# A decoder layer on one core: scores of two groups sooner, output weights on GpSimd's queue, loads behind masks, the last blocks' order pinned

## The chip, the cores and the metric

The kernel runs on one core of a Trainium2 chip. A core has a matrix engine (TensorE, PE in the profile; its weight loads are PEld), VectorE (DVE), ScalarE (ACT), GpSimd (POOL) and SyncE (SP). They run side by side, each through its own list of instructions in order, and wait for each other by semaphores. Transfers are issued by SP, POOL or ACT in the order of their lists and are carried by 16 DMA engines. The metric is the device time of one execution in microseconds. The kernel before takes 1504.59 us, the median of three runs (1503.69 to 1505.47).

## What is computed

One layer of a decoder: 4096 new tokens of one prompt, and 8 samples with 8 tokens each against caches. A norm, one wide projection, three groups of heads, one output projection, a second norm and the residual sum:

```python
h = _rmsnorm(x, g_pre)
z = h @ w_in                                    # 4096+64 tokens, 1024 -> 2816
cb, cc, ch, cg, q, k, v, ag, mq, mg = _split_cols(z)
...
out_a = jax.nn.silu(cg) * cb * conv             # conv of 3 tokens over cc * ch, 256 channels
o_b, new_k, new_v = _window_prompt(q, k, v, sink_g)   # 8 heads, window 128, in blocks of 128 queries
out_b = jax.nn.silu(ag) * o_b
o_c = _mem_attend(mq.reshape(n, t, MEM_HEADS, HEAD_DIM), mem_k, mem_v)   # 4 heads, 256 memory tokens
out_c = jax.nn.silu(mg) * o_c
y = jnp.concatenate([out_a, out_b, out_c], axis=-1) @ w_out
return x + _rmsnorm(y, g_post), new_conv, new_k, new_v
```

All is float32. Each factor is split into a high and a low part of a shorter format, and a product is three passes (high by high, low by high, high by low).

## The kernel before

The input projection runs in three phases over the columns of w_in. Here only phase 2 matters (669 to 955 us): 8 blocks of 520 tokens, and for each block seven products p = 0 to 6 in place of eight (a Strassen-like scheme over a 2 x 2 split). A step is one product of one block; the text counts them n = 7 (b - 1) + p from block 1 on, so n = 30 is block 5, product 2. A step is 36 matmuls of 128 x 260 (line 374). For each step SP loads the tile x (x_5T, x_6B, x_7T, ...: block and place in the scheme), ACT casts it to hi (line 364), DVE takes the difference lo (line 365), and DVE adds the finished product into z (evictions, line 381). DVE also forms gates (line 417) and turns values (vq, line 851).

On these steps third_jobs hangs other work. The prompt's attention is cut into 32 groups of 128 queries, two to a chunk of 256; a chunk has its keys kst, queries q (chunk_load: one load of kst and two of q on GpSimd's queue) and its mix, the gated rows into which the attention is multiplied (load_mix). The first three groups are worked on during phase 2: pieces 0 to 3 are their scores (ws for the window, xs for the memory, on PE; softmax on ACT and DVE), then the turn (a transpose in 32 x 32 squares on DVE and 16 transfers w<-s that move the squares), the masks (four GpSimd instructions on w, into w and wd), and the values (pv on PE). The table EARLY gives the step of each piece, a row to a group.

Then come blocks i = 0 to 32 of attention and output projection, 128 tokens each (32 is the samples): 48 matmuls y<-wo with events hung between them, each at a place (half of the columns, k of 8). Block i holds the scores of group i + 3, its turn, the masks of group i + 2 and, at its start, the values of group i + 1. Behind the matmuls follow the norm (ACT squares, DVE, the root by pow on GpSimd, ACT scales) and the sum with x (xr, on GpSimd). The samples' attention is spread over blocks 26 to 30 by the table sample: sample_window has the stages load and mask, then sws and svnt (scores and the turning of new values) with their softmax, then swt (the turned weights), then swo. Its mask tile smask and the masked weights wd of even groups lie in one slot (wp[0]), which one of them holds at a time.

What sets the order: phases 0 and 1 are written out by hand. From phase 2 on a scheduler orders each engine's instructions by what it takes to be ready first; only what is marked (keep_in_program_order, or everything of an engine while the InOrder flags are set: DVE and PE in all blocks before the last, POOL in blocks 1 and 2, ACT in block 0) stays in the order of the program. Slots of a pool are given to whoever is scheduled first. w_out is loaded by wo_load in eight pairs (wor) into slots that the last weights and tiles of phase 2 leave, and wo_split splits it (ACT casts, DVE or GpSimd subtracts, line 197).

## Time and profile before

| | us |
|---|---|
| median of three runs | 1504.59 |
| the profiled execution | 1505.62 |
| its span, first to last instruction | 1503.9 |
| PE busy in the span | 1470.2 (98%) |
| DVE busy | 1211.9 (81%) |
| ACT busy | 758.0 (50%) |
| POOL busy | 441.8 (29%) |
| mean granted PE clock | 0.992 of full |

Times in the trace count from the first instruction. A row of waits names the engine and the line that stood still, then the instruction or transfer that ended it. Line 66 is a helper through which most instructions of the blocks are recorded, so they are told apart by their tiles. A name such as pv<-w,vh means that pv is written from w and vh; buffer numbers are left out. SPq and POOLq are the issuing queues. The PE clock is granted by the chip in parts of full speed.

### The profile page before, as it was taken

To read this page: it belongs to the slowest core of one execution; us is meant where nothing else is said; L and a number is where in the kernel's file an instruction comes from. 1 tells how busy PE (TensorE), PEld (TensorE's weight loads), DVE (VectorE), ACT (ScalarE), POOL (GpSimd) and SP (SyncE) were. 2 spreads that over 40 slices of the span, in tenths; PEclk is the share of its full clock that TensorE was granted. 3 is DMA by queue.
4 is the path that set the end of the run, shared out by engine and by line. 5 is a ranking of instruction groups with operands and counts; after the bars stand their busy time and mean duration, and the time that the engine had idled before them with its cause. 6 is when DMAs were issued, how large, how long until landed. Compare 5 with 4: busy or idle time off the path is not lost.

```text
span 1503.9 us, 30849 instructions
## 1 busy us (share of the span) xinstructions
PE 1470.2 (98%) x11459; PEld 1343.8 (89%) x11459; DVE 1211.9 (81%) x1889; ACT 758.0 (50%) x1869; POOL 441.8 (29%) x607
## 2 busy tenths in 40 slices
PE   9999999999999999999999999889999999999988
PEld 9999999999999999999999889767777777777756
DVE  6779888899988777797667767969888988889833
ACT  6776566465422222254534435656556566556531
POOL 0223233212300000000003213355665565666531
PEclk9999999999999999999999999999999999999989
DMA  9989999887854333478877988898899988898662
GB/s 258 196 234 227 287 294 266 249 262 264 236 197 165 120 114 115 146 247 290 288 233 210 273 255 261 293 254 213 231 238 239 235 220 214 222 242 211 190 203 78
DMA packets 213756, 337.26 MB, mean 224 GB/s; under 512 B 55270, under 2 KB 126822, under 8 KB 213574
## 3 DMA queue, kind: packets, MB, share of 16 engines
q1 hardware_dynamic: 169973, 259.23, 57.5%
q0 software_dynamic: 42336, 72.91, 20.1%
q10 hardware_dynamic: 1296, 3.15, 0.6%
q8 instruction: 91, 1.49, 0.4%
q14 instruction: 60, 0.48, 0.1%
HBM read 192.48 MB, written 110.15 MB: 201 GB/s over the span
## 4 chain that ended last, share of the span: by engine, by line
PE 77%; DMA 6%; issue 6%; DVE 6%; ACT 2%; SPq 1%; POOL 1%; ACTq 0%; POOLq 0%; DVEq 0%
PE c L374 49%; PE y L66 18%; PE pv L66 4%; PE ws L66 2%; DMA w<-s 1%; PE xs L66 1%; DMA place<-md 1%; PE mem_acc L789 1%; SPq L1234 1%; ACT s L1193 1%; DMA x_5T<-hd_T 1%; DMA wr_3S<-sd6S 1%; DMA o_yp<-xr 1%; DMA vd<-v 1%; DMA x_7B<-hd_B 0%
## 5 line engine op out<-in xcount | busy, mean ns | idle before, releaser
L66 PE MATMUL y<-wo,mh 128*128 128x512 f32 x992 | 319.2, 396 | 0.0
L381 DVE TENSOR_TENSOR z<-c,z 128x520 f32<-128x520 f32 (+1 forms) x308 | 194.5, 644 | 93.7 <-PE c L374 92.5
L66 PEld LDWEIGHTS y<-wo,mh 128*128 128x128 f32 x992 | 187.1, 189 | 52.3 <-DVE wmx L66 5.4
L66 PE MATMUL y<-wo,ml 128*128 128x512 f32 x496 | 194.0, 391 | 0.0
L1193 ACT ACTIVATE s<-s,wnm 128x128 f32<-128x128 f32 x248 | 96.0, 388 | 47.8 <-DVE wnm L66 42.8
L1217 POOL TENSOR_SCALAR s<-s,xrd 128x256 f32<-128x256 f32 x120 | 57.5, 493 | 199.0 <-DVE xrd L66 104.0
L66 PEld LDWEIGHTS y<-wo,ml 128*128 128x128 f32 x496 | 93.6, 189 | 18.3
L1178 ACT COPY s<-ws 128x256 f32<-128x256 f32 x124 | 40.0, 378 | 94.0 <-PE ws L66 70.5
L748 POOL MEMSET negs<- 128x1 f32 x1 | 0.1, 99 | 266.7 <-PE c L374 266.7
L1565 POOL TENSOR_TENSOR xr<-yn,xr 128x1024 f32<-128x1024 f32 x29 | 69.6, 2400 | 21.6 <-ACT yn L1564 21.4
L66 DVE STREAM_TRANSPOSE s<-s 128x1024 f32<-128x1024 f32 x58 | 71.0, 1237 | 3.1 <-POOL s L1217 2.9
L1248 POOL TENSOR_SCALAR_AFFINE_SELECT wd<-w 128x512 f32<-128x512 f32 (+1 forms) x60 | 53.8, 896 | 49.2 <-DMA w<-s 30.7
L1545 ACT ACTIVATE y<-y 128x512 f32<-128x512 f32 (+1 forms) x64 | 37.4, 584 | 51.4 <-DVE yn L66 44.5
L66 DVE TENSOR_TENSOR yn<-y,gpost 128x512 f32<-128x512 f32 x62 | 42.3, 682 | 22.8 <-PE y L66 21.6
L1209 ACT ACTIVATE s<-xs,xnm 128x256 f32<-128x256 f32 x124 | 56.4, 462 | 5.5 <-DVE xnm L1207 4.8
L66 DVE COPY_PREDICATED s<-wmask,ws 128x256 f32<-128x256 uint8 x116 | 45.0, 440 | 15.3 <-ACT s L1178 5.5
L66 PEld LDWEIGHTS ws<-kst,q 64*128 64x128 f32 x696 | 43.1, 186 | 12.9 <-issue 12.9
L66 PE MATMUL ws<-kst,q 64*128 64x256 f32 x696 | 49.1, 287 | 2.7 <-issue 2.7
L383 ACT COPY z<-c 128x520 f32<-128x520 f32 (+1 forms) x44 | 24.4, 554 | 51.9 <-PE c L374 49.3
L1248 POOL TENSOR_SCALAR_AFFINE_SELECT w<-w 128x512 f32<-128x512 f32 x60 | 48.9, 834 | 1.8
L1564 ACT ACTIVATE yn<-yn,yst 128x1024 f32<-128x1024 f32 x31 | 35.7, 1150 | 27.0 <-POOL yst L1558 24.6
L287 ACT ACTIVATE nat<-nat 104x1024 f32<-104x1024 f32 x40 | 42.2, 1055 | 11.4 <-DMA nat<-in_x_p 11.4
(999 smaller groups left out, 5019.1 us busy)
## 6 DMA issues: line engine op xcount, KB each, us to landing
w<-s SPq DMA_DIRECT2D x464, 64.0 KB
q<-qd POOLq DMA_DIRECT2D x32, 768.0 KB, 8.8
xr<-in_x_p SPq DMA_DIRECT2D x32, 512.0 KB
nat<-in_x_p SPq DMA_DIRECT2D x39, 416.0 KB
o_yp<-xr SPq DMA_DIRECT2D x31, 512.0 KB
md<-th POOLq DMA_DIRECT2D x48, 260.0 KB, 6.8
qd<-zh SPq DMA_DIRECT2D x48, 260.0 KB
qd<-z SPq DMA_DIRECT2D x48, 260.0 KB
```

The costliest lines, as they stand in the source:

```text
L66: return (lambda *args, **kw: tc.keep_in_program_order(fn(*args, **kw))) if on else fn
L287: S.activation(t[:RG], t[:RG], AF.Square, accum_out=r[:RG, i : i + 1])
L374: TE.matmul(bank[:, :HW], l, r, start=first and i == 0, stop=last and i == 3 * KH - 1)
L381: add = lambda dst, other: V.tensor_tensor(dst, c, other, op=ALU.add)
L1178: S.copy(to, squares(s3[:, :, P : 2 * P]))
L1193: S.activation(sm[:, h], sm[:, h], AF.Exp, bias=nm[:, h : h + 1], scale=SCALE, accum_out=den[:, h : h + 1])
L1209: S.activation(p[:, i], s[:, i].rearrange("p (a k j) -> p a k j", a=2, k=4), AF.Exp, bias=nm[:, i : i + 1], scale=SCALE, accum_out=den[:, ...
L1217: G.tensor_scalar(p[:, i], p[:, i], rd[:, i : i + 1], 0.5, op0=ALU.mult, op1=ALU.mult)
L1248: G.affine_select(out, src, pattern=[[32 * sign, 2], [0, 8], [sign, 32]], compare_op=op, fill=0.0, base=base * sign, channel_multiplier=-s ...
L1545: square = lambda acc=acc, p=p, c0=c0, c1=c1, end=end: S.activation((psum(2, "sq") if end else acc)[:m, : c1 - c0], acc[:m], AF.Square, sc ...
L1564: tc.keep_in_program_order(S.mul(yn, yn, st[:, 3:4]))
L1565: G.tensor_tensor(self.xr, yn, self.xr, op=ALU.add)
```

## The change

Five things are changed.

1. EARLY: group 0's turn, masks and values come one, two and two steps sooner; all pieces of group 1 three to five steps sooner; those of group 2 six to eight. Chunk 1's load goes from step 29 to step 26.
2. wo_load issues on GpSimd's queue instead of SP's, and the last split goes from GpSimd to DVE.
3. Chunk 3's keys and queries, and chunk 2's mix, are asked for behind the masks of group 3 in block 1; the mix goes from SP's queue to GpSimd's.
4. In blocks 28 to 30 the root and the sum on GpSimd stay in the order of the program.
5. sample_window's second stage goes from the first half of block 28 to its second.

```diff
-        if n == 29:
-            jobs.append(lambda: chunk_load(1))
         for b, at in enumerate(EARLY):
...
+        if n == 26:
+            jobs.append(lambda: chunk_load(1))
...
-    EARLY = ((15, 16, 17, 18, 20, 24, 26), (25, 26, 27, 28, 30, 34, 36), (36, 37, 38, 39, 41, 45))
+    EARLY = ((15, 16, 17, 18, 19, 22, 24), (22, 23, 24, 25, 26, 29, 31), (30, 31, 32, 33, 34, 37))
...
-            DMA.dma_start(wo_raw[j + n], a["w_out"][k + n][:, 512 * h : 512 * h + 512])
+            G.dma_start(wo_raw[j + n], a["w_out"][k + n][:, 512 * h : 512 * h + 512])
...
-        w_split(wo[k][h], wo_raw.pop(j), G if j > 8 and j % 2 else V)
+        w_split(wo[k][h], wo_raw.pop(j), G if j in (9, 11, 13) else V)
...
-            DMA.dma_start(self.mix, md[:, :, self.ts].rearrange("k p n -> p k n"))
+            (G if self.c == 2 else DMA).dma_start(self.mix, md[:, :, self.ts].rearrange("k p n -> p k n"))
...
-        if i in (1, 2):
-            chunk_load(i + 2)
+        if i == 2:
+            chunk_load(4)
...
-                G.tensor_tensor(st[:m, 3:4], st[:m, 3:4], mhalf[:m, 0:1], op=ALU.pow)
+                root = G.tensor_tensor(st[:m, 3:4], st[:m, 3:4], mhalf[:m, 0:1], op=ALU.pow)
+                if 28 <= b < 31:
+                    tc.keep_in_program_order(root)
...
-                    G.tensor_tensor(self.xr, yn, self.xr, op=ALU.add)
+                    total = G.tensor_tensor(self.xr, yn, self.xr, op=ALU.add)
+                    if 28 <= b < 31:
+                        tc.keep_in_program_order(total)
...
-              (27, 0, 3): window, (28, 0, 6): window, (29, 0, 4): window, (30, 0, 3): window}
+              (27, 0, 3): window, (28, 1, 3): window, (29, 0, 4): window, (30, 0, 3): window}
...
-        elif (i + 3) // 2 < NCH - 1:
+        elif 1 < i and (i + 3) // 2 < NCH - 1:
             at(0, 3, lambda: chunks[(i + 3) // 2].load_mix())
         at(1, 1, turn, 2, i + 2)
+        if i == 1:
+            at(1, 1, chunk_load, 3)
+            at(1, 1, lambda: chunks[2].load_mix())
```

How the instructions stand, at three places. At the start of step 39 PE had two pieces of group 2's memory scores between the products; they are gone from there, and the first matmul that needs lo_6T follows the two high ones at once.

ScalarE in steps 45 to 48, before; hi are the casts of the tiles of steps 45 to 48, wo the casts of the output weights:

```order
L364 CAST hi_7T_11766<-x_7T_11644 128x1040
L364 CAST hi_7T_11821<-x_7T_11707 128x1040
L193 CAST wo_0_11783<-wor_11727 128x512
L193 CAST wo_0_11799<-wor_11727 128x512
L193 CAST wo_0_11816<-wor_11743 128x512
L193 CAST wo_0_11843<-wor_11743 128x512
L193 CAST wo_0_11859<-wor_11761 128x512
L193 CAST wo_0_11862<-wor_11761 128x512
L364 CAST hi_7B_11885<-x_7B_11764 128x1040
L193 CAST wo_0_11902<-wor_11879 128x512
L364 CAST hi_7T_11943<-x_7T_11819 128x1040
```

And after:

```order
L364 CAST hi_7T_11771<-x_7T_11649 128x1040
L193 CAST wo_0_11788<-wor_11732 128x512
L193 CAST wo_0_11804<-wor_11732 128x512
L193 CAST wo_0_11821<-wor_11748 128x512
L364 CAST hi_7T_11826<-x_7T_11712 128x1040
L193 CAST wo_0_11843<-wor_11748 128x512
L193 CAST wo_0_11859<-wor_11766 128x512
L193 CAST wo_0_11862<-wor_11766 128x512
L364 CAST hi_7B_11885<-x_7B_11769 128x1040
L193 CAST wo_0_11902<-wor_11879 128x512
```

Three of the six weight casts now stand ahead of the tile of step 46 (hi_7T) and three behind it, ahead of hi_7B of step 47. The tiles' loads on SP's queue, which stood around the weights' loads, follow each other directly; the weights' loads stand on GpSimd's queue behind group 2's masks and ahead of the splits and of q and kst of chunk 2.

GpSimd from group 3's last weights on, before (L1217 and L66 TENSOR_SCALAR are the memory weights of groups 3 and 4, wd and w the masks of group 3):

```order
L66 TENSOR_TENSOR yst_12175<-yst_12175,mhalf 128x1
L66 TENSOR_TENSOR xr_12168<-yn_12174,xr_12168 128x1024
L66 DMA kst_12423<-qd 128x2x384
L66 DMA q_12425<-qd 128x6x256 x2
L66 TENSOR_SCALAR s_12351<-s_12351,xrd_0_12450 128x2x4x32 x2
L66 TENSOR_SCALAR s_12351<-s_12351,xrd_1_12458 128x2x4x32 x2
L66 AFFINE_SELECT wd_12508<-w_12334 128x512
L66 AFFINE_SELECT wd_12508<-w_12334 64x512
L66 AFFINE_SELECT w_12334<-w_12334 128x2x256 x2
```

And after:

```order
L66 TENSOR_SCALAR s_12351<-s_12351,xrd_0_12445 128x2x4x32 x2
L66 TENSOR_SCALAR s_12351<-s_12351,xrd_1_12453 128x2x4x32 x2
L66 AFFINE_SELECT wd_12502<-w_12334 128x512
L66 AFFINE_SELECT wd_12502<-w_12334 64x512
L66 AFFINE_SELECT w_12334<-w_12334 128x2x256 x2
L66 DMA kst_12507<-qd 128x2x384
L66 DMA q_12509<-qd 128x6x256 x2
L66 DMA place<-md 128x8x256
```

Keys and queries of chunk 3 have moved from the front of group 4's weights to behind group 3's masks, and the mix (place<-md) has come to this queue behind them.

GpSimd in blocks 28 and 29, before: the cast of smask, weights of group 31, masks of group 30, root (yst) and sum (xr) of block 28, root of block 29, masks of group 31 around the sum of block 29:

```order
L1426 CAST smask<-smraw 128x768
L1217 TENSOR_SCALAR s_18017<-s_18017,xrd_0_18112 128x2x4x32 x2
L1217 TENSOR_SCALAR s_18017<-s_18017,xrd_1_18120 128x2x4x32 x2
L1248 AFFINE_SELECT wd_18238<-w_17970 128x512
L1248 AFFINE_SELECT wd_18238<-w_17970 64x512
L1248 AFFINE_SELECT w_17970<-w_17970 128x2x256 x2
L1558 TENSOR_TENSOR yst_18015<-yst_18015,mhalf 128x1
L1565 TENSOR_TENSOR xr_17677<-yn_18014,xr_17677 128x1024
L1558 TENSOR_TENSOR yst_18294<-yst_18294,mhalf 128x1
L1248 AFFINE_SELECT wd_18387<-w_18248 128x512
L1248 AFFINE_SELECT wd_18387<-w_18248 64x512
L1565 TENSOR_TENSOR xr_17893<-yn_18293,xr_17893 128x1024
```

And after:

```order
L1248 AFFINE_SELECT wd_18193<-w_17970 128x512
L1248 AFFINE_SELECT wd_18193<-w_17970 64x512
L1248 AFFINE_SELECT w_17970<-w_17970 128x2x256 x2
L1426 CAST smask<-smraw 128x768
L1558 TENSOR_TENSOR yst_18015<-yst_18015,mhalf 128x1
L1567 TENSOR_TENSOR xr_17677<-yn_18014,xr_17677 128x1024
L1248 AFFINE_SELECT wd_18387<-w_18203 128x512
L1248 AFFINE_SELECT wd_18387<-w_18203 64x512
L1248 AFFINE_SELECT w_18203<-w_18203 128x2x256 x2
L1558 TENSOR_TENSOR yst_18294<-yst_18294,mhalf 128x1
```

The cast of smask now stands behind the masks of group 30, where the slot makes it wait for PE's last product of group 30's values, and the masks of group 31 stand ahead of block 29's root.

## The prediction

> **What bounds the kernel now.** I read the page first, then the waits of TensorE (PE), then the time in stretches, then single stretches of each queue.
>
> ```profile
> PE 1470.2 (98%) x11459; PEld 1343.8 (89%) x11459; DVE 1211.9 (81%) x1889; ACT 758.0 (50%) x1869; POOL 441.8 (29%) x607
> ```
>
> PE is busy for 98% of the span and no other engine comes near, and the change neither adds nor removes a matmul. So it can only move the time in which PE stands still, and the time in which PE runs slowly. Its waits that this change can reach lie in two places. From 800 to 1000 us, steps 20 to 48 of the input projection and the first blocks (waiting engine and line, what ended the wait, us in total, times, longest):
>
> ```profile
> PE pv L66 <- DMA w<-s: 4.8, 1, 4.8
> PE ws L66 <- issue: 2.7, 1, 2.7
> PE c L374 <- DVE lo_5B L365: 2.4, 1, 2.4
> PE c L374 <- DVE lo_7B L365: 1.5, 1, 1.5
> PE c L374 <- DVE lo_5T L365: 1.5, 2, 0.8
> PE c L374 <- ACT hi_7B L364: 0.9, 1, 0.9
> PE c L374 <- DVE lo_6T L365: 0.7, 1, 0.7
> PE c L374 <- DVE lo_7T L365: 0.6, 1, 0.6
> ```
>
> and from 1420 to 1466 us, the last blocks:
>
> ```profile
> PE pv L66 <- POOL w L1248: 5.9, 1, 5.9
> PE svnt L66 <- ACT s L1209: 0.7, 1, 0.7
> ```
>
> Between the two PE is full (second row below), while the stretch of the early groups is the one where the DMA engines are busiest for long (columns: window, length, busy time and count of PE, PEld, DVE, ACT, POOL, then PE clock, DMA share, GB/s):
>
> ```profile
> 800.00:880.00 80.00, 76.09 (x631) 73.26 (x630) 58.97 (x96) 33.44 (x71) 27.78 (x51) 0.98 0.91 267
> 1000.00:1424.00 424.00, 422.77 (x3063) 332.19 (x3061) 376.01 (x659) 252.53 (x920) 248.93 (x317) 1.00 0.89 226
> ```
>
> Each longer wait is paid a second time: behind it the granted clock falls to a half. The same view of PE alone, cut at the places where the clock changes (window, length, PE busy, PE clock, DMA share, GB/s):
>
> ```profile
> 871.09:874.51 3.42, 3.42 (x18) 0.53 1.12 278
> 939.36:942.77 3.41, 1.81 (x13) 1.00 1.03 389
> 942.77:946.19 3.42, 2.65 (x12) 0.53 1.03 380
> 946.19:949.60 3.41, 3.41 (x18) 0.50 0.36 120
> 993.97:997.39 3.42, 2.92 (x22) 0.53 0.74 208
> 1427.47:1430.88 3.41, 3.41 (x13) 0.52 0.80 232
> 1458.19:1461.60 3.41, 0.48 (x3) 0.52 0.11 44
> 1461.60:1465.00 3.40, 3.40 (x18) 0.50 0.44 139
> ```
>
> The clock changes on a grid of 3.41 us. A piece of the grid with only 1.81 us of PE work, 1.6 idle, is followed by one at half clock. PE work done at half clock costs half its busy time extra.
>
> **What each place loses today.** Wait plus half of the slow work: steps 30–33: 2.4 + 1.5 + 1.7 = 5.6; step 39: 0.7; steps 46–47: 0.6 + 0.9 + 1.5 + (2.65 + 3.41)/2 = 6.0; scores of group 4: 2.7; values of group 3: 4.8 + 1.5 = 6.3; sample window: 0.7 + 1.7 = 2.4; values of group 31: 5.9 + (0.48 + 3.40)/2 = 7.8. Together 31.5 us.
>
> **The change part by part.**
>
> *Earlier scores.* Group 1 moves by three steps or more, group 2 by six, group 0's masks and values by two. Their DVE and ACT work leaves steps 30–33, so the waits for lo_5T and lo_5B there (5.6) and lo_6T (0.7) go. Something takes its place. In step 39 VectorE has the same order today (eviction, turned values, then lo_6T), and PE waits so little because two pieces of group 2's scores stand ahead:
>
> ```profile
> 903.96 0.62 PE L1046 MATMUL xs<-mk,q 64*128 64x256 f32 x6
> 905.24 0.39 PE L374 MATMUL c<-lo_6T,w_0S 128*128 128x260 f32 x1 [0.66 <-DVE lo_6T L365]
> ```
>
> These move to step 33, and without them the wait grows to 0.66 + 2 × 0.62 = 1.9, say 2.1 (between 0.7 and the 2.4 of lo_5B, nearest to the sum); 1.6 us idle in one piece was enough above, so one piece at half clock follows, 1.7. In step 36 lo_6B comes behind evictions and both transposes of group 2; between 0 and 2.4 I take 0.7, as for lo_6T. Gain 6.3 − 4.5 = 1.8, ends −1 and 6.3. GpSimd's 16 turn transfers now run sooner:
>
> ```profile
> 810.79 6.99 POOL L1234 DMA_DIRECT2D w<-s  x14 [5.61 <-DVE s L1229]
> ...
> 824.19 1.54 POOL L1248 TENSOR_SCALAR_AFFINE_SELECT wd<-w 128x512 f32<-128x512 f32 x2 [4.04 <-DMA w<-s]
> ```
>
> They take 13.4 us to the masks. The first two matmuls of step 24, behind which the values of group 0 now stand, are
>
> ```profile
> 820.76 0.29 PE L374 MATMUL c<-hi_4T,w_0S 128*128 128x260 f32 x1
> 820.88 0.28 PE L374 MATMUL c<-lo_4T,w_0S 128*128 128x260 f32 x1
> ```
>
> A step has 36 such matmuls 0.12 us apart, 4.3 us. Issued one step sooner the transfers end at about 820 and the masks (824.19 to about 827 today) at 823, against PE at 821 to 824 within the step: 0 to 2 us of wait, I take 0. Chunk 1's load (two q, one kst on the same queue) is moved ahead of group 1's turn and three steps sooner; nobody needs it before step 30.
>
> *Output weights on GpSimd.* SyncE's queue today:
>
> ```profile
> 925.11 1.67 SPq L525 DMA_DIRECT2D x_7T<-hd_T  x1
> 926.86 5.72 SPq L909 DMA_DIRECT2D wor<-in_w_out  x6
> 932.63 0.44 SPq L525 DMA_DIRECT2D x_7B<-hd_B  x1
> ```
>
> The tile of step 47 (x_7B) stands behind six weight issues. After the change it follows x_7T directly, 5.7 us sooner, and the first six weight loads wait for step 42 only, so that ScalarE's weight casts no longer all stand between hi_7T and hi_7B and need not wait for their loads. What is left of 6.0 lies between 0 and 6.0; three casts and three splits still come ahead of hi_7B and lo_7B, so I leave 1.0 and gain 5.0. GpSimd waits in these issues for slots, but only q2, kst2 and three splits are behind them, and q2 waits for the end of step 48 in any case. One of the splits moves from GpSimd to VectorE. I cost it at nothing, since the 2.7 us wait for chunk 2's keys, which no part of the change touches, comes right behind and covers it; without that cover it costs its own length, at most.
>
> [...] If what holds x_7T and x_7B is the DMA engines (share 1.03 in two rows above), this part gains nothing: that is the first rival.
>
> *Chunk 3's loads and chunk 2's mix behind masks 3.* Today SyncE issues group 3's turn in one stretch:
>
> ```profile
> 972.56 17.53 SPq L1234 DMA_DIRECT2D w<-s  x16
> ```
>
> Among SyncE's waits from 965 to 1000 us, and then on PE, stand
>
> ```profile
> SPq L1234 <- DMA place<-md: 3.9, 1, 3.9
> ```
>
> ```profile
> 994.47 1.97 PE L66 MATMUL pv<-w,mv 128*64 128x128 f32 x16 [4.79 <-DMA w<-s]
> ```
>
> Of the 17.53 us of issuing, 3.9 are a wait for the mix load, issued just ahead. Without it the issues end at 986.2. The wait of PE ended 4.4 us after the last issue; 4.4 behind 986.2 is 990.6, against PE's turn at 989.7: 0.9 left, short of the 1.6 that slowed the clock. Gain 6.3 − 0.9 = 5.4, ends 3 and 6.3. The moved loads (kst3, two q3, mix) now wait on GpSimd for masks 3, about one block later than today; a block lasts about 16 us (424 us, 26 blocks, second row of the stretches), group 6's scores need them in the next, the mix a little later. I cost them at nothing; the cover is that block's products, and if the two q land late PE waits for them, 0 to 3.
>
> *Last blocks.* Sample window's products move to the second half of block 28: the wait for svnt (0.7) goes, and its 1.7 at half clock, since no idle time adds to these small products: 2.4, ends 0 and 2.4. Group 31's masks no longer stand behind block 29's root and sum, and its turn goes ahead of the sample's softmax on DVE, so the wait for them goes with its slow piece, 7.8:
>
> ```profile
> 1461.12 1.97 PE L66 MATMUL pv<-w,vh 128*64 128x256 f32 x8 [5.87 <-POOL w L1248]
> ```
>
> But a new wait comes. The sample's mask tile and group 30's wd share one slot. wd30 now takes it first, so the cast of the mask waits until PE has read wd30, at the end of group 30's values. Behind the cast stand root 28, sum 28 and masks 31; behind the softmax stands PE with swt. The rows of today, on PE, for the mask, and on DVE the first and last of the softmax (ScalarE's part lies between them):
>
> ```profile
> 1438.77 0.66 PE L66 MATMUL pv<-wd,vh 64*64 64x256 f32 x8
> ...
> 1442.24 1.04 PE L66 MATMUL swt<-ident,ssm 128*128 128x128 f32 x8
> ```
>
> ```profile
> L1426 POOL CAST smask<-smraw x1: 823/823/823, 1421.7 to 1421.7; 128x768 uint8<-128x768 f32 x1
> ```
>
> ```profile
> 1429.80 0.65 DVE L66 COPY_PREDICATED_SCALAR ssm<-smask,negs 128x384 f32 x1 [1.20 <-ACT ssm L1445]
> ...
> 1434.99 1.01 DVE L66 TENSOR_SCALAR ssm<-ssm,swrd 128x192 f32<-128x192 f32 x4
> ```
>
> From the end of pv (1439.4) to swt PE has 2.8 us of work. The chain takes 0.8 (cast), 1429.80 to 1434.99 = 5.2, and a quarter of 1.01: 6.3. PE waits 3.5 us, and one piece at half clock adds 1.7. For masks 31 I add to the 6.3 an estimate of 10 us for block 28's norm, root and sum and the four masks: they end some 16 us behind pv. PE comes to group 31's masked values 1461.12 − 5.87 − 1439.4 = 15.8 us behind pv, plus the new 5.2: in time by some 5 us. Gain 7.8 − 5.2 = 2.6, ends 0 and 7.8.
>
> [...]
>
> **Sum.** 1.8 + 5.0 + 5.4 + 2.4 + 2.6 = 17.2. The profiled execution took 1505.62 us, 1.0 above the median of 1504.59; 1505.6 − 17.2 = 1488.4, or 1487.4 against the median. I say 1487. With all lower ends at once the gain is 2, less 3 for late q; with all upper ends it is 28.8: 1476 to 1506.
>
> **Rivals.**
> 1. The DMA engines, not the queue, hold x_7T and x_7B: 5.0 is not gained, 1492 to 1493. For it: share 1.03 there. Against: group 2's megabyte leaves this stretch, and the weights start earlier.
> 2. The new waits of steps 36 and 39 are absorbed (order says who stands ahead, not when it is ready): 4.5 more, 1483, or 1479 where the clock behind swt holds too and chunk 2's keys come sooner.
> 3. Slower: GpSimd's turns land late in the busiest stretch (0.91). Values of groups 0 and 1 now stand five steps (21.5 us) behind the turn instead of six, and PE waits in order. Were the 16 transfers to take 22 us instead of 13.4, each would hold PE some 8 us and cost 3.4 in clock: 23 us, 6 more than the sum, 1510. It decides from about 20 us per turn. Against: the added traffic is one group's 16 × 64 KB, 4 us at 267 GB/s.
> 4. Nothing: each removed wait is handed on to the next in-order wait, 1503 to 1506.
>
> **Chances.** As summed (1483 to 1491) 0.50; rival 1 or the like with q3 late too (1491 to 1500) 0.21; rival 2 (1478 to 1483) 0.13; nothing 0.04; slower 0.12. The range 1479 to 1500 leaves out under 0.2. The measurement tells 0.2%, 3 us, from no change: faster 0.84, same 0.04, slower 0.12.
>
> **What would show it.** Right: the rows for pv behind w<-s and behind w L1248 gone or under 1 us; no lo_5B wait; a new wait of PE swt for DVE ssm of 3 to 4 us with half clock behind it; POOL's cast waiting for PE pv. Wrong: a row of PE pv behind POOL in steps 24 or 31 (rival 3), hi_7B still behind a DMA (rival 1), PE ws waiting for q3 in block 3. A swt that does not wait would make my account of the last blocks false, and the time some 5 us better.

## The result, and the profile after

The changed kernel takes 1503.96 us (median of 12 runs, 1499.29 to 1507.75) against 1504.21 us before in the same session (12 runs, 1500.93 to 1506.79): a ratio of 0.9998, with a 95% interval from 0.9985 to 1.0011. No difference, where 17 us less were predicted. The profiled execution took 1499.29 us (span 1497.6), the lowest of its twelve; the one before took 1505.62, near the top of its own. So a trace tells here where time goes, and sizes come from medians. One execution of part 2 alone (1785.34 us), one of the run on the mask's slot (1584.02) and one of the kernel before (6706.53) lie far above the rest and count in the medians and run counts below, but not in the ratios; without them the first two medians are 1509.36 and 1499.46.

The first line of the page after, engine by engine, is nearly the one of before:

```profile
PE 1467.0 (98%) x11459; PEld 1341.6 (90%) x11459; DVE 1207.6 (81%) x1890; ACT 757.6 (51%) x1869; POOL 448.4 (30%) x623
```

TensorE's waits over the whole span of the changed kernel (what ended the wait, us in total, times, longest):

```profile
PE ws L66 <- issue: 4.3, 1, 4.3
PE swt L66 <- DVE ssm L66: 3.6, 1, 3.6
PE c L374 <- ACT hi_6T L364: 3.1, 1, 3.1
PE pv L66 <- DMA smraw<-in_smask: 2.0, 1, 2.0
PE ws L66 <- ACT y L66: 2.0, 1, 2.0
...
PE ws L1046 <- DVE place L1291: 1.4, 2, 1.0
...
PE c L374 <- DVE lo_6T L365: 0.9, 1, 0.9
...
PE c L374 <- DVE lo_6B L365: 0.8, 1, 0.8
...
PE c L374 <- DVE lo_7T L365: 0.7, 2, 0.4
```

Every wait that the change was aimed at is gone: no lo_5B (2.4 before), no lo_7B (1.5), no pv behind w<-s (4.8) and none behind w L1248 (5.9). Others have come or grown. The view names what came last by the profile, which need not be the cause. Behind "ws <- issue" stand chunk 2's keys (in the trace of before kst is issued at 959.62 us, lands 11.6 us later, and TensorE goes on at 971.31). The sample mask's load in the pv row has nothing to do with these values, which are group 4's; GpSimd's masks for them start only at 1007.10 us, after a wait of 1.70 us for a transfer. In this trace the granted clock is a half from 904.00 to 907.41 us, 968.86 to 975.68, 1009.82 to 1013.23 and 1439.89 to 1446.72: each 3.41 us or twice that, and 18, 10 and 125 times 3.41 apart. TensorE in pieces of that grid (window, length, PE busy, PE clock, DMA share, GB/s):

```profile
904.00:907.41 3.41, 3.00 (x14) 0.50 0.79 164
968.91:972.32 3.41, 1.45 (x14) 0.50 0.98 366
972.32:975.73 3.41, 3.41 (x31) 0.51 0.30 76
1006.41:1009.82 3.41, 1.43 (x26) 1.00 1.24 372
1009.82:1013.23 3.41, 3.41 (x26) 0.50 1.54 372
1439.91:1443.32 3.41, 2.24 (x10) 0.50 0.91 258
1443.32:1446.73 3.41, 3.41 (x21) 0.50 0.59 144
```

Four places ahead of the last block still bring a slow clock, two of them for two pieces. In the prediction's own currency (wait plus half of the slow work, us; in the trace of before the matmuls of the projection follow each other 0.22 us apart at half clock, at 871.50 and 871.72 us, and 0.12 apart at full, at 874.85 and 874.97, so that 45% of the slow time is extra there):

| place | before | predicted to be left | in the trace after |
|---|---|---|---|
| steps 30–33 | 5.6 | 0 | 1.4 (two waits ahead of scores) |
| step 36 | 0 | 0.7 | 0.8 |
| step 39 | 0.7 | 3.8 | 3.1 + 0.9 + 1.5 = 5.5 |
| steps 46–47 | 6.0 | 1.0 | 0.7 |
| scores of group 4 | 2.7 | 2.7 | 4.3 + 2.0 + (1.45 + 3.41)/2 = 8.7 |
| values of group 3 | 6.3 | 0.9 | 0 |
| values of group 4 | 0 | 0 | 2.0 + 1.7 = 3.7 |
| sample window, svnt and swt | 2.4 | 5.2 | 3.6 + (2.24 + 3.41)/2 = 6.4 |
| values of group 31 | 7.8 | 0 | 0 |
| sum | 31.5 | 14.3 | 27.2 |

Three rows make nearly all of the miss of 12.9 us: the scores of group 4 (6.0 more than predicted), the values of group 4 (3.7) and step 39 (1.7). The sum says 4.3 us less than before for this one execution, and it was 6.3 below the profiled one of before. The median of the changed kernel is 4.7 above its profiled execution, and what the other executions lose in addition no trace here shows.

### The profile page after: what moved, and what is told of

Same layout as the page of the kernel before. It is cut to its first block, busy times and chain, and to the rows that moved or that the text cites. A ratio compares the mean times of both kernels' runs of the same rounds, so it can differ in the third digit from the quotient of the medians.

```text
span 1497.6 us, 30845 instructions
## 1 busy us (share of the span) xinstructions
PE 1467.0 (98%) x11459; PEld 1341.6 (90%) x11459; DVE 1207.6 (81%) x1890; ACT 757.6 (51%) x1869; POOL 448.4 (30%) x623
## 4 chain that ended last, share of the span: by engine, by line
PE 78%; DMA 7%; DVE 6%; issue 4%; POOL 2%; SPq 2%; ACT 1%; ACTq 0%; DVEq 0%; POOLq 0%
PE c L374 48%; PE y L66 19%; PE pv L66 5%; PE ws L66 2%; DMA w<-s 1%; PE y L1537 1%; PE xs L66 1%; PE mem_acc L789 1%; DMA x_7T<-hd_T 1%; SPq L1234 1%; DMA gpost<-in_gpost 1%; DVE s L66 1%; DMA vd<-v 1%; DMA wr_2A<-in_w_in 0%; DMA smraw<-in_smask 0%
## 5 line engine op out<-in xcount | busy, mean ns | idle before, releaser
L66 PE MATMUL y<-wo,mh 128*128 128x512 f32 x992 | 318.7, 396 | 0.0
L66 PEld LDWEIGHTS y<-wo,mh 128*128 128x128 f32 x992 | 186.5, 188 | 52.7 <-DVE wnm L66 5.0
L66 PE MATMUL y<-wo,ml 128*128 128x512 f32 x496 | 193.6, 390 | 0.0
L1217 POOL TENSOR_SCALAR s<-s,xrd 128x256 f32<-128x256 f32 x120 | 57.7, 494 | 183.3 <-DVE xrd L66 106.1
L66 PEld LDWEIGHTS y<-wo,ml 128*128 128x128 f32 x496 | 93.5, 188 | 18.2
L66 DVE STREAM_TRANSPOSE s<-s 128x1024 f32<-128x1024 f32 x58 | 70.9, 1236 | 5.1 <-POOL s L1217 2.7
L1248 POOL TENSOR_SCALAR_AFFINE_SELECT wd<-w 128x512 f32<-128x512 f32 (+1 forms) x60 | 55.6, 926 | 49.5 <-DMA w<-s 28.8
L66 DVE TENSOR_TENSOR yn<-y,gpost 128x512 f32<-128x512 f32 x62 | 42.3, 683 | 29.5 <-PE y L66 22.7
L66 PEld LDWEIGHTS ws<-kst,q 64*128 64x128 f32 x696 | 44.3, 189 | 17.2 <-issue 14.2
L66 PE MATMUL ws<-kst,q 64*128 64x256 f32 x696 | 50.6, 291 | 6.6 <-issue 4.3
L66 DVE COPY_PREDICATED s<-wmask,ws 128x256 f32<-128x256 uint8 x116 | 44.9, 440 | 10.2 <-ACT s L1178 7.7
L1248 POOL TENSOR_SCALAR_AFFINE_SELECT w<-w 128x512 f32<-128x512 f32 x60 | 46.2, 790 | 1.8
```

The source lines that it names most:

```text
L66: return (lambda *args, **kw: tc.keep_in_program_order(fn(*args, **kw))) if on else fn
L1217: G.tensor_scalar(p[:, i], p[:, i], rd[:, i : i + 1], 0.5, op0=ALU.mult, op1=ALU.mult)
L1248: G.affine_select(out, src, pattern=[[32 * sign, 2], [0, 8], [sign, 32]], compare_op=op, fill=0.0, base=base * sign, channel_multiplier=-s ...
```

## The experiments

In the expectations groups are counted from one: the "third group" is group 2 of the code, whose scores move by six steps, and the fifth is group 4. Ratios are to the kernel before, run on the same chip in the same session; the sessions' medians of before were 1503.23, 1504.52, 1503.92 and 1502.58 us. A difference to the changed kernel or between two sessions is one of medians, unless the text says ratio.

**Each part alone.** First, which part pays and which costs. Part 1, the earlier scores:

```diff
-        if n == 29:
-            jobs.append(lambda: chunk_load(1))
...
+        if n == 26:
+            jobs.append(lambda: chunk_load(1))
-    EARLY = ((15, 16, 17, 18, 20, 24, 26), (25, 26, 27, 28, 30, 34, 36), (36, 37, 38, 39, 41, 45))
+    EARLY = ((15, 16, 17, 18, 19, 22, 24), (22, 23, 24, 25, 26, 29, 31), (30, 31, 32, 33, 34, 37))
```

> Only the table EARLY and chunk 1's load are changed. Theory 1 (each part's gain is its own, as the prediction summed): 1.8 us faster than before. Theory 2 (a removed wait is handed to the next thing that PE needs, a transfer): the waits for lo_5T and lo_5B go (5.6 us with their slow piece), but group 2's 16 turn transfers stand in the way of x_6T for step 39: a wait of PE for hi_6T of some 3 us with a slow piece behind it, and no difference beyond 2 us in the time.

1504.67 us (12 runs), ratio 1.0002 [0.9988, 1.0016]: nothing, as theory 2 had it. The waits for lo_5T and lo_5B are gone, and at step 39 TensorE waits for a load instead:

```profile
PE c L374 <- ACT hi_6T L364: 2.5, 1, 2.5
...
PE c L374 <- DVE lo_6T L365: 1.4, 1, 1.4
```

Two more new waits, each with a piece at half clock behind it, stand ahead of early scores (1.78 us at 826.16 us and 1.70 at 873.02). Steps 46 and 47, which this part was not meant to change, have no wait at all any more, although x_7B still stands behind six weight issues in SyncE's queue:

```profile
934.49 3.18 SPq L909 DMA_DIRECT2D wor<-in_w_out  x6
937.93 0.43 SPq L525 DMA_DIRECT2D x_7B<-hd_B  x1
```

The six issues take 3.18 us here and 5.72 before, and x_7B goes out 12.3 us ahead of TensorE's arrival at step 47 (950.19), where before it was 8.2 (932.63, arrival 940.78).

Part 2, the output weights:

```diff
-            DMA.dma_start(wo_raw[j + n], a["w_out"][k + n][:, 512 * h : 512 * h + 512])
+            G.dma_start(wo_raw[j + n], a["w_out"][k + n][:, 512 * h : 512 * h + 512])
...
-        w_split(wo[k][h], wo_raw.pop(j), G if j > 8 and j % 2 else V)
+        w_split(wo[k][h], wo_raw.pop(j), G if j in (9, 11, 13) else V)
```

> Only the output weights' loads go to GpSimd's queue, and one split to VectorE. Theory 1: the waits of steps 46 and 47 (6.0 us) shrink to 1.0, 5 us faster. Theory 2: they shrink, but PE then comes 5 us sooner to group 4's scores, whose keys do not come sooner: the wait of ws there grows from 2.7 to 5 or more, and the time is the same within 2 us.

1510.57 us (9 runs), ratio 1.0045 [1.0027, 1.0063]: slower by 6.8 us by the ratio, where 5 less were predicted and neither theory had a loss. Its waits from 940 to 984 us name the cause:

```profile
ACT y L66 <- DVE yn L66: 12.7, 2, 10.2
DVE yn L66 <- DMA gpost<-in_gpost: 11.9, 1, 11.9
...
PE ws L66 <- ACT y L66: 10.3, 1, 10.3
```

VectorE, on its first block, waits 11.9 us for gpost, the weights of the output norm; ScalarE, which squares the same block, waits for VectorE; and TensorE, in the second half of group 4's scores, waits 10.3 us for ScalarE and is slow (6.77 us of work in a stretch of 17.1 at half clock, from 972.1 us). Nothing in the change names gpost. But with sixteen issues gone from SyncE's queue, the remaining ones are put in another order. The one issue of gpost in the kernel before, in this one, and in the full change (line, queue, out and in, ns, time of issue):

```profile
L1587 SPq DMA_DIRECT2D gpost<-in_gpost x1: 400/400/400, 953.9 to 953.9; - x1
```

```profile
L1587 SPq DMA_DIRECT2D gpost<-in_gpost x1: 422/422/422, 969.7 to 969.7; - x1
```

```profile
L1591 SPq DMA_DIRECT2D gpost<-in_gpost x1: 819/819/819, 958.4 to 958.4; - x1
```

Before, it stands in the middle of the qd stores; with part 2 alone behind all of them, behind chunk 1's mix and two blocks' inputs; in the full change behind all the qd stores, and behind the first loads of chunk 2. There the engines move 378 and 377 GB/s (960 to 965 and 965 to 970 us), and VectorE still waits for it:

```profile
DVE yn L66 <- DMA gpost<-in_gpost: 4.1, 1, 4.1
```

Part 2 alone also shows what it needs part 1 for. x_7B follows x_7T directly, as predicted, and goes out 14.4 us ahead of step 47 (TensorE comes at 940.13):

```profile
924.28 1.39 SPq L525 DMA_DIRECT2D x_7T<-hd_T  x1
925.72 0.85 SPq L525 DMA_DIRECT2D x_7B<-hd_B  x1
```

Yet steps 46 to 48 wait 4.6 us in all (0.70 for hi_7T, 0.89 for lo_7T, 1.06 for lo_7B and, at step 48, 1.90 for lo_7T), where the kernel before waits 3.0. Group 2's turn is still on its way there: GpSimd issues the first weight load, then the turn, and the other weights behind it (start, us):

```profile
918.29 0.60 POOL L909 DMA_DIRECT2D wor<-in_w_out  x1 [6.10 <-PE c L374]
918.89 3.44 POOL L1234 DMA_DIRECT2D w<-s  x7
...
930.35 0.50 POOL L1234 DMA_DIRECT2D w<-s  x1 [2.51 <-DMA w<-s]
931.16 1.66 POOL L909 DMA_DIRECT2D wor<-in_w_out  x3 [0.32 <-DMA w<-s]
```

In the full change the turn's issues are over by 895 us. So what took the waits of steps 46 and 47 away was group 2's turn leaving this stretch, more than x_7B's place in the queue. Whether it is the turn's transfers that hold the tiles, or the late weights and the splits behind them, these runs don't separate.

Part 3, chunk 3's loads and chunk 2's mix:

```diff
-            DMA.dma_start(self.mix, md[:, :, self.ts].rearrange("k p n -> p k n"))
+            (G if self.c == 2 else DMA).dma_start(self.mix, md[:, :, self.ts].rearrange("k p n -> p k n"))
...
-        if i in (1, 2):
-            chunk_load(i + 2)
+        if i == 2:
+            chunk_load(4)
...
+        if i == 1:
+            at(1, 1, chunk_load, 3)
+            at(1, 1, lambda: chunks[2].load_mix())
```

> Only chunk 3's keys and queries and chunk 2's mix go behind the masks of group 3. Theory 1: the wait of pv for group 3's turn (4.8 us and a slow piece) goes, 5.4 us faster. Theory 2: the wait goes, but the 2.9 MB now travel with group 4's turn, and pv of group 4 waits some 2 us with a slow piece behind: 2 to 3 us faster.

1504.45 us (12 runs), ratio 1.0006 [0.9992, 1.002]: nothing again. The wait of group 3's values is gone; the next group's values wait instead, as theory 2 had it, but its 2 to 3 us did not come. The second row is a later wait, of group 6:

```profile
1008.46 1.09 PE L66 MATMUL pv<-w,mv 128*64 128x128 f32 x16 [2.75 <-ACT y L1545]
1045.53 1.97 PE L66 MATMUL pv<-w,mv 128*64 128x128 f32 x16 [3.84 <-ACT y L1545]
```

Group 4's turn did not come later for the moved loads. GpSimd's masks behind it start at 1009.28 us before and at 1006.67 here:

```profile
1009.28 1.52 POOL L66 TENSOR_SCALAR_AFFINE_SELECT wd<-w 128x512 f32<-128x512 f32 x2 [4.05 <-DMA o_yp<-xr]
```

```profile
1006.67 1.52 POOL L66 TENSOR_SCALAR_AFFINE_SELECT wd<-w 128x512 f32<-128x512 f32 x2 [2.86 <-DMA w<-s]
```

They gain 2.6 us, but TensorE, which no longer stands behind group 3, comes 6.2 us sooner (1005.71 against 1011.90). Before, the first masks were ready 1.1 us ahead of it (1009.28 + 1.52 against 1011.90). The 3.84 us of group 6, with a piece at half clock behind them, stand in no other trace here, and their cause was not followed.

Parts 4 and 5, the pinned order of the last blocks and the sample window's later products:

```diff
+                if 28 <= b < 31:
+                    tc.keep_in_program_order(root)
...
-(28, 0, 6): window
+(28, 1, 3): window
```

> Only the last blocks are changed (order of root and sum, place of the sample window's products). Both theories: the 5.9 us wait of pv for GpSimd's masks goes, a wait of swt for ssm of 3.5 us comes. Theory 1: 4.8 us faster, since svnt's wait and its slow piece go too. Theory 2: half of it, 2 to 3 us, since two slow pieces follow the wait of swt.

1500.95 us (12 runs), ratio 0.9978 [0.9967, 0.999]: 3.3 us less by the ratio, the only part that gains by itself, between the two theories. Its waits are the predicted ones, svnt and group 31's values gone and a new one for swt, with one piece at half clock behind it (at 1447.3 us):

```profile
PE swt L66 <- DVE ssm L66: 3.6, 1, 3.6
```

The four differences add up to 4.7 us more (0.02 + 0.45 + 0.06 − 0.22 = 0.31%), all together gave −0.02%. With intervals of some ±0.14% each this is barely clear of noise; that the parts depend on one another is seen better in the waits, at steps 46 to 48 and behind gpost.

**Is it gpost?** Part 2 alone once more, and the full change, with gpost issued by GpSimd ahead of chunk 2's loads:

```diff
-    DMA.dma_start(gpost, a["gpost"].partition_broadcast(P))
...
+    G.dma_start(gpost, a["gpost"].partition_broadcast(P))
     chunks[1].load_mix()
     chunk_load(2)
```

> The kernel with the output-weight part alone took 1510.57 us against 1503.23 before, and in its trace TensorE stands 10.3 us in the middle of the fifth group's scores, while VectorE waits 11.9 us for the load of the output norm's weights (gpost), which SyncE issued only at 969.71 us (953.91 before). Here the same part, with that one load issued by GpSimd ahead of chunk 2's loads. Theory (the late gpost load carries the whole loss): VectorE's wait and the 10.3 us are gone, gpost lands before 962 us, and the time is 1500 to 1505 us (the 6.8 us come back). Rival 1 (the loss is the queue on GpSimd: chunk 2's loads start late behind sixteen weight loads): gpost ahead of them makes them later still, the time stays at 1509 to 1513 us. Rival 2 (the DMA engines are full between 960 and 975 us, whatever the order): some 3 us of the 10.3 stay, as a longer wait for kst, 1505 to 1508 us.

1501.06 us (10 runs), ratio 0.998 [0.9962, 0.9999]. One load on another queue is worth 0.65% by the ratios, 9.8 us. In its trace gpost is issued at 956.5 us, and the row of that view on its landing reads

```profile
DMA to landing us min/median/max: 5.0/5.0/5.0
```

VectorE no longer waits for it, and the 10.3 us are gone. The wait for kst stays at 3.7. The first theory held; rival 1 (queue on GpSimd) and rival 2 (full DMA engines) did not.

> The changed kernel with the gpost load issued by GpSimd ahead of chunk 2's loads instead of by SyncE behind the qd stores. In the changed kernel VectorE waits 4.1 us for gpost and TensorE 2.0 us behind it (972 us), after 4.3 us for kst; five grid pieces of half clock follow. Theory (gpost is the second half of the new wait at the fifth group's scores): the 2.0 us go, the 4.3 us shrink by up to 1.3 us (0.5 MB less in the DMA engines at 390 GB/s), and about 1.7 us of half clock with them: 1499 to 1501 us against 1504. Rival (the wait only moves on to the next one in order, the values of the fifth group): those values wait 4 us or more, and the time stays within 1.5 us of 1504.

1500.68 us (11 runs), ratio 0.9974 [0.9962, 0.9987]: 3.3 us below the changed kernel. The second wait of group 4's scores is gone, as expected; the first did not shrink (4.5 us), so that part of the expectation was wrong. Nor are the pieces at half clock behind these waits five in the changed kernel: they are two, from 968.86 to 975.68 us.

**Is it the third group's turn?** The full change with group 2's scores three steps sooner instead of six:

```diff
-(30, 31, 32, 33, 34, 37))
+(33, 34, 35, 36, 37, 40))
```

> The changed kernel with the third group's scores three steps sooner than before instead of six (its turn through DRAM at about 902 us instead of 886 us). In the changed kernel step 39 waits 3.1 + 0.9 us for x_6T, which SyncE issued at 896.3 us (891.5 before), behind the vn and qd stores and next to the turn's sixteen DMAs. Theory (the turn next to the x_6T loads makes them late): x_6T is issued by 893 us, both waits and one piece of half clock go, 1498 to 1501 us. Rival (the x_6T loads are late because TensorE gained some microseconds on the DMA engines, which are over 0.9 busy from 885 to 910 us with or without the turn): the waits at step 39 stay at 2.5 us or more, or come at step 42 for x_7B instead, and the time stays within 1.5 us of 1504.

1498.88 us (11 runs), ratio 0.996 [0.9946, 0.9975]: 5.1 us below the changed kernel. What made x_6T late is seen in SyncE's queue, in the changed kernel

```profile
884.50 0.54 SPq L180 DMA_DIRECT2D qd<-zh  x1
887.57 0.32 SPq L180 DMA_DIRECT2D qd<-z  x1
887.98 0.40 SPq L180 DMA_DIRECT2D qd<-zh  x1
889.41 3.58 SPq L855 DMA_DIRECT2D vn<-vq  x4
...
896.31 1.36 SPq L525 DMA_DIRECT2D x_6T<-hd_T  x1
```

and before:

```profile
886.20 1.95 SPq L855 DMA_DIRECT2D vn<-vq  x4
...
891.50 0.64 SPq L525 DMA_DIRECT2D x_6T<-hd_T  x1
```

SyncE waits for results of VectorE (z, vq), which has group 2's scores to do just there; the issues also take longer (the four of vn 3.58 us against 1.95, x_6T 1.36 against 0.64), and the load that step 39 needs comes behind both. It is issued 3.7 us before TensorE comes to hi_6T (903.05 − 3.06 = 899.99), in the run with the later scores 6.6 us before TensorE comes to the same step (898.99, and 907.57 − 2.02). The time expected for the issue, by 893 us, was wrong in absolute terms, and only half of the wait went: hi_6T waits no more, lo_6T still does, with a slow piece:

```profile
907.57 0.55 PE L374 MATMUL c<-lo_6T,w_0S 128*128 128x260 f32 x1 [2.02 <-DVE lo_6T L365]
```

That is the 2.1 us which the prediction had for this place. Whether the turn's DMAs or VectorE's order carry more of the delay, the run doesn't separate, since both move.

**Is it the mask's slot?** The full change with the mask in spare columns of its own source tile, so that nothing ties the cast to group 30's second scores tile:

```diff
-        msk = wp[0].tile([P, 8 * CT], U8, tag="wd", name="smask")[:, : 4 * 192].rearrange("p (a n) -> p a n", a=4)
...
+        smraw = work("smraw")
+        msk = smraw[:, 4 * 192 : 5 * 192].bitcast(U8).rearrange("p (a n) -> p a n", a=4)
```

> The changed kernel with the sample window's mask cast into spare columns of its own source tile instead of into the slot of a group's second scores tile, so that the cast on GpSimd no longer waits for that group's values on TensorE. In the changed kernel TensorE waits 3.6 us for the window's scores (swt) at 1441 us, and has half clock in the 3.4 us before it and 3.4 us behind. Theory (the slot is the cause): the cast starts 7 us or more sooner, the swt wait is below 0.5 us, and 4 to 6 us go: 1498 to 1500 us against 1504. Rival (the wait is for VectorE's own row of work, which the pinned order put there): the cast starts sooner but swt still waits over 2 us and the time is within 1.5 us of 1504.

1499.7 us (6 runs), ratio 0.9963 [0.995, 0.9975]: 4.3 us less. The cast in the changed kernel and here, on GpSimd:

```profile
1434.58 0.82 POOL L1426 CAST smask<-smraw 128x768 uint8<-128x768 f32 x1 [4.72 <-PE pv L66]
```

```profile
1436.71 0.81 POOL L1427 CAST smraw<-smraw 128x768 uint8<-128x768 f32 x1
```

It waits no longer, and swt, which starts at 1444.88 here, follows the work ahead of it without a wait; the clock is full there. The two starts lie in executions of different length, so they are compared with TensorE's arrival at swt: the cast starts 8.2 us ahead of it here, and 2.9 in the changed kernel (1441.08 − 3.63 − 1434.58). That is 5.3 us sooner, not the 7 or more expected, and enough.

**All three repairs, and then one step further.**

> The changed kernel with all three repairs that were tried apart: gpost issued by GpSimd (1500.68 us alone), the third group's scores three steps sooner instead of six (1498.88), the window's mask outside the scores' slot (1499.70); the changed kernel itself took 1503.96. Theory (three separate waits, each of which took back what a part of the change had gained): the gains of 3.3, 5.1 and 4.3 us add up to 12.7, so 1490 to 1493 us. Rival (what is gained before chunk 2's loads is handed on to the wait for them, which stands at 4.5 to 4.7 us in all three traces): only the largest of the first two and the mask's gain show, 1494 to 1497 us, with the wait for kst over 5 us.

1490.39 us (6 runs, 1488.58 to 1496.05), ratio 0.992 [0.99, 0.9939]: 13.6 us below the changed kernel, where the three gains alone add up to 12.7. By the ratios it is 0.78% against 0.24 + 0.38 + 0.35 = 0.97%, 11.7 against 14.6 us. Within what can be measured they add, and the rival's 1494 to 1497 us are out. TensorE's longest waits that are left:

```profile
PE ws L66 <- DMA xr<-in_x_p: 4.1, 1, 4.1
PE pv L66 <- ACT y L1546: 3.1, 4, 2.1
PE c L374 <- DVE lo_6T L365: 2.0, 1, 2.0
```

The wait for chunk 2's keys is the largest. Is it held up by the megabyte of mix beside it?

```diff
-            (G if self.c == 2 else DMA).dma_start(self.mix, md[:, :, self.ts].rearrange("k p n -> p k n"))
+            (G if self.c in (1, 2) else DMA).dma_start(self.mix, md[:, :, self.ts].rearrange("k p n -> p k n"))
...
-    chunks[1].load_mix()
     chunk_load(2)
+    chunks[1].load_mix()
```

> The same kernel as the one with all three repairs, and chunk 1's load of the mixed values (1 MB) issued by GpSimd behind chunk 2's three loads instead of by SyncE beside them. In the three traces TensorE waits 4.5 to 4.7 us for chunk 2's kst and q2, which land 10.5 to 11.6 us after their issue, while the engines move 360 to 394 GB/s. Theory (the DMA engines share themselves among the queues, so a megabyte on another queue holds these loads up): behind them in the same queue it comes after them, they land up to 2.6 us sooner (1 MB at 390 GB/s), the wait is 1.5 to 3 us, and the time 2 to 4 us below the kernel with the three repairs. Rival 1 (the loads are late because their sources, the qd stores, are): the wait stays over 4 us and the time within 1.5 us of that kernel. Rival 2 (the mixed values become the late transfer): the values of the fourth group wait 3 us or more, same time or slower.

1491.3 us (5 runs), ratio 0.9919 [0.9902, 0.9935]: no change, and the wait stays at 4.4 us. So not the theory; the first rival forecast this outcome. The mix load is issued at 964.6 us here and at 963.1 with the three repairs, 3 us before the wait ends, and so 7 us or more behind the loads that are waited for (from 952 to 956) in both. The rival's own cause, the late stores, was not shown. In both traces the engines move about 380 GB/s (378 and 390) from 960 to 968 us.

**What did part 3 give away?** The kernel before with the mix alone behind the masks, chunk 3's loads left where they were:

```diff
-            DMA.dma_start(self.mix, md[:, :, self.ts].rearrange("k p n -> p k n"))
+            (G if self.c == 2 else DMA).dma_start(self.mix, md[:, :, self.ts].rearrange("k p n -> p k n"))
...
+        if i == 1:
+            at(1, 1, lambda: chunks[2].load_mix())
```

> The kernel before with half of the part on chunk 3 and chunk 2's mixed values: the load of the mixed values goes behind the fourth group's masks on GpSimd, chunk 3's own loads stay where they were (ahead of that group's turn). The whole part alone took 1504.45 us against 1503.23 before; its trace has no wait at the fourth group's values any more (4.8 us before) but 2.8 us at the fifth group's, whose turn through DRAM then travels with chunk 3's loads. Theory (the moved loads took the gain back): the fifth group's values wait less than 1 us, the fourth group's too, and the time is 1499 to 1501 us. Rival (the wait is handed on in order, loads or no loads): the fifth group's values wait 2 us or more again and the time is 1503 to 1505 us.

1500.42 us (12 runs), ratio 0.9979 [0.9967, 0.999], where the whole part has 1.0006. Leaving the loads alone is worth 4 us. The waits beside them don't show where: the values of group 4 wait no more, but those of group 3 do, nearly as long as group 4's did with the loads moved (2.75):

```profile
990.35 1.09 PE L66 MATMUL pv<-w,mv 128*64 128x128 f32 x16 [2.50 <-ACT y L1545]
```

Group 4's masks start at 1006.93 us here, no sooner than with the loads moved. TensorE stands still 25.8 us in this whole trace and 32.3 in that of the whole part; most of the difference lies at group 6's values (0.5 against 3.8 us) and, where no edit reaches, behind 1415 us (3.6 against 6.5). So the time fits the theory, but its cause is not shown.

Last, the same in the kernel with all three repairs:

```diff
-        if i == 2:
-            chunk_load(4)
+        if i in (1, 2):
+            chunk_load(i + 2)
...
-            at(1, 1, chunk_load, 3)
```

> The kernel with all three repairs (1490.39 us, 0.992 of before), and chunk 3's own loads back ahead of the fourth group's turn, as in the run with half of that part (1500.42 against 1504.45 us with the whole part). In the trace with the three repairs the fifth group's values still wait 2.1 us at 1004 us, with a piece of half clock behind them. Theory (the moved loads cost there what they cost alone): that wait falls below 1 us and 2 to 4 us more go, 1486.5 to 1489 us, 0.988 to 0.990 of before. Rival (in this kernel the fourth group's values, whose masks stand behind those loads on GpSimd again, wait instead): they wait 2 us or more and the time is 1489.5 to 1493 us.

1492.36 us (6 runs, 1486.59 to 1494.39), ratio 0.9919 [0.9899, 0.9939]: the same as with the loads moved. Neither account holds whole: group 3's values don't wait, but group 4's still do,

```profile
1007.73 1.09 PE L66 MATMUL pv<-w,mv 128*64 128x128 f32 x16 [1.71 <-ACT y L1546]
```

though chunk 3's loads have landed by 989.6 us. The mix load (issued at 989.9) and chunk 4's loads still go out beside group 4's turn. So moving the loads costs some 4 us where part 3 stands alone and nothing that can be measured in the repaired kernel; by which wait it costs them, and what holds group 4's values in the repaired kernel, is open.

## Why the prediction was wrong, step by step

The forecast gain did not come because three places were costed at nothing or not looked at, and they took back what the removed waits had given. It is the fourth rival (1503 to 1506 us, chance 0.04), partly in its form: group 3's wait was handed on to group 4, and the wait for chunk 2's keys grew. The rest was lost to transfers that came to stand later in a queue (gpost, x_6T).

- *Earlier scores, predicted 1.8, alone nothing.* The waits of steps 30 to 33 went as predicted, and step 36 costs the 0.7 that was given (0.8). The step that failed is "the wait grows to 0.66 + 2 × 0.62 = 1.9, say 2.1" at step 39: lo_6T alone was looked at, and where its source comes from was not. The order that stood in the prediction was VectorE's; the one that decided was SyncE's, where x_6T's issue stands behind results of VectorE. Three steps instead of six gives 5.1 us back. This part also did what was credited to the next one: alone it leaves no wait at steps 46 and 47.
- *Output weights, predicted 5.0, alone 6.8 us slower.* Two steps failed. The first is "The tile of step 47 (x_7B) stands behind six weight issues" as the account of the 6.0 us: with those issues out of the way steps 46 to 48 still wait 4.6 us, and with them in place and group 2's turn gone (part 1 alone) steps 46 and 47 don't wait. In the full change the waits went. The second is "the 2.7 us wait for chunk 2's keys, which no part of the change touches". It grew to 4.3 us, since TensorE came 4.4 us sooner (968.55 − 4.34 against 971.31 − 2.69) and the keys only 2.8. A wait of 2.0 came behind it, because gpost had moved in SyncE's queue. The move was to be read in the order of that queue, but only the rows around x_7B were read there. Gpost back in time is worth 3.3 us in the full change and 9.8 in the part alone.
- *The first rival.* Its outcome, that the second part gains nothing at x_7T and x_7B, held for the part alone. Its cause, full DMA engines, is not shown: in part 1 alone they are as full (share 1.03 from 930 to 945 us), and nothing waits. The engines also move as much with gpost on either queue: in part 2 alone 379 GB/s (960 to 968 us), and with gpost issued early by GpSimd 376 (968 to 973 us).
- *Chunk 3's loads and the mix, predicted 5.4, alone nothing.* The wait behind the mix went as predicted. The step that failed is "Gain 6.3 − 0.9 = 5.4", which ends at group 3: the values of group 4 had no term. Their masks were ready 1.1 us ahead of TensorE before, TensorE came 6.2 us sooner and the masks 2.6, so 2.75 us of the gain were lost at the next values in order (2.0 with a slow piece in the full change). "I cost them at nothing", of the moved loads, was wrong by some 4 us in the part alone and by nothing measurable in the repaired kernel; the wait that carries it is not shown. With the loads left where they were the part gains 3.5 us.
- *Last blocks, predicted 5.0, alone 3.3.* Right in each wait: svnt and group 31's values gone, swt at 3.63 us (3.5 predicted), for the mask's slot. Mis-sized in this trace was the slow clock behind swt, two pieces (2.24 and 3.41 us of work) instead of one: 2.8 instead of 1.7. That is how the wait fell on the grid: the same 3.6 us brought one piece in the traces of parts 4 and 5 alone, of gpost and of the third group's turn. The run without the shared slot takes 4.3 us less, against the 5.2 of the prediction and the 6.4 of the trace.
- *The third rival* (turns on GpSimd late in steps 24 or 31) did not come about: no such row of pv behind GpSimd in the trace after.
- *The clock.* "Each longer wait is paid a second time" has an exception in the trace of before: the 2.7 us for chunk 2's keys fell across two pieces of the grid (1.62 and 1.06 us idle, from 966.84 and from 970.25 us), and the clock stayed full. That 1.6 us idle in one piece are enough was not shown either: cut at the clock's own changes, the piece with 1.81 us of work has 1.64 (939.53 to 942.94 us), so 1.77 idle. After, the piece from 1006.41 us has 1.43 us of work, 1.98 idle, and the next one is at half clock.

## What to carry to other kernels

When instructions are taken out of an in-order queue, read again where every other transfer of that queue has come to stand, above all the ones needed once and at a fixed time: a load that nobody edited went 16 us further back and cost more than the edit could gain. When a wait is removed, look at the next one in the same engine's order: how long its tile stands ready, and whether it comes sooner too. A wait for a tile needs its source followed back to the queue that loads it, and a tile's place in a queue is shown to be the cause only when the wait goes with it and stays without. Undoing the suspects one by one in the changed kernel found 12 us that the parts measured alone would not have shown.

## What the hardware showed that was not expected

The size of the effect of one load of half a megabyte: issued at 956.5 us it landed in 5.0 us; issued at 969.7 us, with the engines at 394 GB/s, VectorE went on at 977.8, and with half clock behind the wait the whole kernel was 0.65% longer, 9.8 us.

The spread: twelve executions of one kernel, with the same instructions, lie up to 8.6 us apart (part 1 alone). The waits differ with them: lo_7B waits 1.5 us in the trace of before and 2.2 us in that of parts 4 and 5 alone, whose edits lie some 480 us later. A single trace here can't size a change of a few microseconds.

Part of the spread is how a wait falls on the clock's grid. In the traces of before and after, from 700 to 1478 us, eight pieces at full clock have 1.77 to 3.41 us idle, and each is followed by a piece at half clock; behind the others at full clock, with 1.62 us idle or less, the clock stays full but for one place (before, from 1424.23 us, 0.69 idle). The wait of 2.4 us for lo_5B fell into one piece in the trace of before (2.36 idle) and brought a slow piece; in that of part 3 alone it fell across two (1.51 and 0.84) and brought none. By the prediction's measure, half of a slow piece of 3.41 us, the same wait is worth 1.7 us more or less by this alone.
